# Resizing the phases and shortening the bank-by-bank tails of a streamed weight-gradient matmul, with smaller early transfers and a longer warm-up

**Chip, cores, metric.** One NeuronCore of one Trainium2 chip. The metric is the device time of one execution in microseconds (us). The "span" of a profile is the same execution seen from the core's first instruction, 1.7 to 1.8 us shorter than the device time here. All runs named below were of the fast state, with correct results.

## The reference

```python
batch, m, k, n = 16, 512, 1024, 768
input       = randn(batch, m, k)      # float32
grad_output = randn(batch, m, n)      # float32
grad_weight = einsum('bmk,bmn->kn', input, grad_output)   # float32, 1024 x 768
```

It is one matmul with a contraction over 16 x 512 = 8192 rows. Both inputs are read once, 58.7 MB of float32.

## The kernel before

The contraction is cut into 64 slices of 128 rows. A slice is x (128 x 1024) and g (128 x 768); GpSimd's DMAs cast both to bf16 on the way into SBUF (the page: 58.72 MB read from HBM, 28.97 MB moved by their queue). The output has 8 row blocks k; each is computed in a "wide" part of 512 columns, which fills one of the kernel's 8 PSUM buffers (a "bank" in the code), and a "narrow" part of 256. With 8 of them, the wide parts of all 8 blocks can stand in PSUM at once, but not the narrow ones beside them. So slices are grouped in phases: within a phase all wide matmuls come first, slice by slice as slices land ("streamed"), then the narrow ones, block by block, and each finished bank is added into an SBUF accumulator.

```python
PHASES = [4, 8, 10, 14, 18, 10]        # slices in each phase
BANKWISE = [1, 2, 4, 6, 10, 10]        # of these, the last ones done bank by bank
WARMUP = 20
# [cut: setup]
    nc.sync.dma_start(out=g0f, in_=G[0:P, 0:NA])              # slice 0 comes as float32
    nc.scalar.dma_start(out=x0f[:, 0:NA], in_=X[0:P, 0:NA])   # NA = 512
    nc.sync.dma_start(out=x0f[:, NA:K], in_=X[0:P, NA:K])
    for i in range(WARMUP):                                   # runs while slice 0 is on its way
        nc.tensor.matmul(wps[:, 0:P], warm, warm, start=(i == 0), stop=(i == WARMUP - 1))
# [cut: slice 0 is cast to bf16 by VectorE and ScalarE in blocks of 256 columns]
# [cut: slices 1 to 3: g's wide columns, x; then the narrow columns of slices 0 to 3 in one transfer]
    def load_pair(s):                                         # from slice 4 on: two slices a transfer
        gt = xg.tile([P, 2, N], bf16, name="gt")              # 20 buffers
        xt = xg.tile([P, 2, K], bf16, name="xt")
# [cut: two DMAs issued by GpSimd]
    for ph, C in enumerate(PHASES):
        load_upto(s0 + (PHASES[ph + 1] if not last else 0))
        streamed = slices[: C - BANKWISE[ph]]
        rest = slices[C - BANKWISE[ph] :]
        for i, s in enumerate(streamed):                      # wide, slice by slice
            for k in range(KS):
                nc.tensor.matmul(banks[k], xblk[s](k), gwide[s], start=(i == 0), stop=False)
        for k in range(KS):                                   # wide, bank by bank
            for i, s in enumerate(rest):
                nc.tensor.matmul(bank, xblk[s](k), gwide[s], ...)
            evacuate(acc[:, k, 0:NA], bank, ...)              # VectorE adds the bank into acc
        for k in range(KS):                                   # narrow, bank by bank
            for i, s in enumerate(slices):
                nc.tensor.matmul(bank[:, 0:NB], xblk[s](k), gnarrow[s], ...)
            evacuate(acc[:, k, NA:N], bank[:, 0:NB], ...)
```

The bankwise tail spreads the evacuations: with R slices in it, banks finish R x 0.216 us apart. Its price is that block 0 wants all R slices at once.

## Time and profile before

Device time 184.51 us in the median of three runs (184.46 to 185.03); the profiled execution took 183.78, with a span of 182.0.

| from the profile before | |
|---|---|
| wide matmul, start to start | 0.216 us |
| narrow matmul, start to start | 0.109 us |
| all matmuls, 512 wide and 512 narrow | 166.5 us |
| a pair of slices in the DMA queue | 4.31 us |
| first matmul of slice 0 | 4.98 us |
| longest waits of TensorE for a slice | near 21, 26, 30 and 121 us |
| last matmul | 178.4 us |

How to read it: a timeline row gives start, duration, engine, source line, what it writes from what, and how many instructions are merged; in square brackets the idle time before it and what ended that. A wide matmul is shown with 379 ns, but the next one starts 216 ns after it; the distance between starts is what counts. The prediction below shows the lines.

### The profile page before, as it was taken

The page shows a single profiled execution, that of the slowest core. Times are in us where ns is not written, and L with a number is a line of the kernel's source. Part 1 is how long each engine was busy: PE and PEld are TensorE (multiplying, and loading weights), DVE is VectorE, ACT ScalarE, POOL GpSimd, SP SyncE. Part 2 cuts the span into 40 slices and gives each one's busy share as a digit, 9 for nine tenths or more (in the row PEclk, how much of TensorE's full clock was granted, in tenths as well). Part 3 has the DMA queues.
Part 4 walks back from the last instruction along what each step waited for, and adds up shares of the span by engine and source line. Part 5 has one row for each costly group of instructions (what it writes and reads, how often), then busy time and mean ns, then how long its engine had stood idle before and what let it go on. Part 6 is the DMA issues. An engine that isn't in the chain of part 4 may idle for free.

```text
span 182.0 us, 2421 instructions
## 1 busy us (share of the span) xinstructions
PE 171.2 (94%) x1032; PEld 102.2 (56%) x1044; DVE 49.1 (27%) x92; ACT 5.6 (3%) x11; POOL 36.1 (20%) x71
## 2 busy tenths in 40 slices
PE   5999878999999999999999999969999999999992
PEld 4347323684435884444488844424448886444781
DVE  0126001950038430004542200013332211333331
ACT  2116000000000000000000000000000000000000
POOL 7642222222222222222222222222000000000000
PEclk9999999999999999999999999999999999999999
DMA  5999999999999999999999999999999100333342
GB/s 175 200 210 213 213 213 211 214 213 211 215 211 213 213 213 214 212 212 212 214 213 212 211 213 214 214 212 214 212 214 210 22 4 0 115 115 115 121 142 86
DMA packets 12778, 33.05 MB, mean 182 GB/s; under 512 B 1376, under 2 KB 3296, under 8 KB 12768
## 3 DMA queue, kind: packets, MB, share of 16 engines
q0 software_dynamic: 10032, 28.97, 81.0%
q1 hardware_dynamic: 2592, 3.67, 5.7%
q10 hardware_dynamic: 144, 0.26, 0.5%
q8 instruction: 8, 0.13, 0.3%
q14 instruction: 2, 0.02, 0.0%
HBM read 58.72 MB, written 3.15 MB: 340 GB/s over the span
## 4 chain that ended last, share of the span: by engine, by line
DMA 62%; PE 31%; POOL 3%; issue 2%; DVE 0%; POOLq 0%
DMA xt<-in_input_dram 62%; PE bank L145 18%; PE bank L156 13%; POOL gw L81 1%; POOL x L82 1%; POOL gn L86 0%; POOL gt L96 0%; DVE acc L122 0%; POOLq L178 0%
## 5 line engine op out<-in xcount | busy, mean ns | idle before, releaser
L122 DVE TENSOR_TENSOR acc<-bank,acc 128x512 f32<-128x512 f32 (+1 forms) x80 | 43.8, 557 | 117.6 <-PE bank L145 84.4
L145 PE MATMUL bank<-gt,xt 128*128 128x512 bf16 x251 | 56.3, 379 | 2.7 <-DMA xt<-in_input_dram 2.3
L156 PE MATMUL bank<-gt,xt 128*128 128x256 bf16 x480 | 53.2, 273 | 0.0
L139 PE MATMUL bank<-gt,xt 128*128 128x512 bf16 x218 | 48.9, 379 | 2.0 <-DMA xt<-in_input_dram 1.7
L156 PEld LDWEIGHTS <-xt 128*128 128x128 bf16 x480 | 47.0, 98 | 6.5
L145 PEld LDWEIGHTS <-xt 128*128 128x128 bf16 x256 | 24.7, 98 | 33.4 <-DMA xt<-in_input_dram 4.4
L139 PEld LDWEIGHTS <-xt 128*128 128x128 bf16 x224 | 21.8, 98 | 27.6 <-DMA xt<-in_input_dram 2.5
L97 POOL DMA_DIRECT2D xt<-in_input_dram x30 | 15.9, 531 | 49.0 <-DMA xt<-in_input_dram 47.8
L96 POOL DMA_DIRECT2D gt<-in_grad_output_dram x30 | 15.9, 531 | 40.0 <-DMA gt<-in_grad_output_dram 35.8
L117 DVE COPY acc<-bank 128x512 f32<-128x512 f32 (+1 forms) x8 | 4.1, 553 | 8.1 <-PE bank L145 7.2
L139 PEld LDWEIGHTS <-x 128*128 128x128 bf16 x24 | 2.8, 119 | 6.0 <-issue 2.8
L139 PE MATMUL bank<-g,x 128*128 128x512 bf16 x8 | 3.6, 631 | 1.6 <-ACT x L69 1.6
L139 PE MATMUL bank<-gw,x 128*128 128x512 bf16 x16 | 4.0, 408 | 0.0
L119 ACT COPY acc<-bank 128x512 f32<-128x512 f32 (+1 forms) x8 | 3.5, 486 | 9.0 <-PE bank L145 7.4
L156 PE MATMUL bank<-gn,x 128*128 128x256 bf16 x32 | 3.7, 272 | 0.0
L156 PEld LDWEIGHTS <-x 128*128 128x128 bf16 x32 | 3.1, 98 | 0.6
L64 PE MATMUL bank<-warm 128*128 128x128 bf16 x20 | 2.3, 313 | 1.1 <-DVE warm L61 1.1
L64 PEld LDWEIGHTS <-warm 128*128 128x128 bf16 x20 | 2.0, 147 | 1.1 <-DVE warm L61 1.1
L81 POOL DMA_DIRECT2D gw<-in_grad_output_dram x3 | 1.8, 594 | 0.8 <-POOLq L178 0.8
L145 PE MATMUL bank<-gw,x 128*128 128x512 bf16 x7 | 1.8, 379 | 0.1
L82 POOL DMA_DIRECT2D x<-in_input_dram x3 | 1.7, 556 | 0.0
L68 DVE CAST g<-g0f 128x512 bf16<-128x512 f32 x1 | 0.5, 477 | 3.3 <-DMA g0f<-in_grad_output_dram 3.3
(12 smaller groups left out, 4.8 us busy)
## 6 DMA issues: line engine op xcount, KB each, us to landing
xt<-in_input_dram POOLq DMA_DIRECT2D x30, 512.0 KB, 17.0
gt<-in_grad_output_dram POOLq DMA_DIRECT2D x30, 384.0 KB, 17.0
out_dram<-acc SPq DMA_DIRECT2D x8, 256.0 KB, 2.0
out_dram<-acc SPq DMA_DIRECT2D x8, 128.0 KB, 1.7
x<-in_input_dram POOLq DMA_DIRECT2D x3, 256.0 KB, 6.5
gw<-in_grad_output_dram POOLq DMA_DIRECT2D x3, 128.0 KB, 5.8
g0f<-in_grad_output_dram SPq DMA_DIRECT2D x1, 256.0 KB, 3.6
x0f<-in_input_dram ACTq DMA_DIRECT2D x1, 256.0 KB, 3.8
```

The lines of the kernel that those rows point to most:

```text
L64: nc.tensor.matmul(wps[:, 0:P], warm, warm, start=(i == 0), stop=(i == WARMUP - 1))
L68: nc.vector.tensor_copy(out=g0, in_=g0f)
L81: nc.gpsimd.dma_start(out=gt, in_=G[s * P : (s + 1) * P, 0:NA])
L82: nc.gpsimd.dma_start(out=xt, in_=X[s * P : (s + 1) * P, :])
L96: nc.gpsimd.dma_start(out=gt, in_=G[rows, :].rearrange("(p r) n -> p r n", r=2))
L97: nc.gpsimd.dma_start(out=xt, in_=X[rows, :].rearrange("(p r) k -> p r k", r=2))
L117: nc.vector.tensor_copy(out=dst, in_=src)
L119: nc.scalar.copy(out=dst, in_=src)
L122: nc.vector.tensor_add(out=dst, in0=src, in1=dst)
L139: nc.tensor.matmul(banks[k], xblk[s](k), gwide[s], start=(i == 0), stop=False)
L145: nc.tensor.matmul(bank, xblk[s](k), gwide[s], start=(i == 0 and not streamed), stop=(i == len(rest) - 1),)
L156: nc.tensor.matmul(bank[:, 0:NB], xblk[s](k), gnarrow[s], start=(i == 0), stop=(i == C - 1),)
```

## The change

The intent: let each phase take as many slices as DMA has ready by then, want no slice early, get the first slices in small pieces and in the order of need, and have the clock up when they come.

- PHASES and BANKWISE: all phases from the third on but the last keep one slice for the bankwise pass.
- Slices 1 to 11 come without their narrow columns, which follow once for each of the first two phases; slices 12 to 21 come one by one; pairs start at 22, with 14 pair buffers instead of 20.
- Slice 0's x in pieces of 256, 256 and 512 columns; 30 warm-up matmuls instead of 20.

```diff
-PHASES = [4, 8, 10, 14, 18, 10]
-
-BANKWISE = [1, 2, 4, 6, 10, 10]
-WARMUP = 20
+PHASES = [5, 7, 10, 15, 18, 9]
+
+BANKWISE = [1, 2, 1, 1, 1, 9]
+
+SPLIT = 2
+
+PAIRED = 22
+WARMUP = 30
[cut]
+    QX = 256
     g0f = head.tile([P, NA], f32, name="g0f")
-    x0f = head.tile([P, K], f32, name="x0f")
+    x0f = [head.tile([P, w], f32, name=f"x0f{i}") for i, w in enumerate((QX, QX, NA))]
     nc.sync.dma_start(out=g0f, in_=G[0:P, 0:NA])
-    nc.scalar.dma_start(out=x0f[:, 0:NA], in_=X[0:P, 0:NA])
-    nc.sync.dma_start(out=x0f[:, NA:K], in_=X[0:P, NA:K])
+    nc.scalar.dma_start(out=x0f[0], in_=X[0:P, 0:QX])
+    nc.scalar.dma_start(out=x0f[1], in_=X[0:P, QX : 2 * QX])
+    nc.sync.dma_start(out=x0f[2], in_=X[0:P, NA:K])
[cut: the casts of slice 0 read the new pieces; ScalarE's comes first]
+    def load_split(slices):
+        n = len(slices)
+        for s in slices:
+            if s == 0:
+                continue
+            gt = early.tile([P, NA], bf16, name=f"gw{s}")
+            xt = early.tile([P, K], bf16, name=f"x{s}")
+            nc.gpsimd.dma_start(out=gt, in_=G[s * P : (s + 1) * P, 0:NA])
+            nc.gpsimd.dma_start(out=xt, in_=X[s * P : (s + 1) * P, :])
[cut]
+        gn = early.tile([P, n, NB], bf16, name=f"gn{slices[0]}")
+        rows = slice(slices[0] * P, (slices[0] + n) * P)
+        nc.gpsimd.dma_start(out=gn, in_=G[rows, NA:N].rearrange("(s p) n -> p s n", p=P))
[cut]
+    def load_rows(s, R):
+        gt = xg.tile([P, R, N], bf16, name=f"gt{R}", bufs=10 if R == 1 else 14)
+        xt = xg.tile([P, R, K], bf16, name=f"xt{R}", bufs=10 if R == 1 else 14)
[cut]
+    def load_phase(ph):
[cut]
+        if ph < SPLIT:
+            load_split(list(range(loaded, loaded + PHASES[ph])))
+            loaded += PHASES[ph]
+            return
+        upto = sum(PHASES[: ph + 1])
+        while loaded < upto:
+            R = 2 if loaded >= PAIRED else 1
+            load_rows(loaded, R)
+            loaded += R
```

More of the change, by code (lines that the diff above doesn't have):

```diff
@@ L41 @@
     head = ctx.enter_context(tc.tile_pool(name="head", bufs=1))
-    xg = ctx.enter_context(tc.tile_pool(name="xg", bufs=20))
+    early = ctx.enter_context(tc.tile_pool(name="early", bufs=1))
+    xg = ctx.enter_context(tc.tile_pool(name="xg", bufs=13))
     accp = ctx.enter_context(tc.tile_pool(name="accp", bufs=1))
@@ L66 @@
     g0 = head.tile([P, NA], bf16, name="g0")
-    x0 = [head.tile([P, 256], bf16, name=f"x0_{i}") for i in range(4)]
+    x0 = [head.tile([P, QX], bf16, name=f"x0_{i}") for i in range(4)]
+    nc.scalar.copy(out=x0[0], in_=x0f[0])
     nc.vector.tensor_copy(out=g0, in_=g0f)
-    nc.scalar.copy(out=x0[0], in_=x0f[:, 0:256])
-    nc.vector.tensor_copy(out=x0[1], in_=x0f[:, 256:512])
-    nc.vector.tensor_copy(out=x0[2], in_=x0f[:, 512:768])
-    nc.scalar.copy(out=x0[3], in_=x0f[:, 768:1024])
+    nc.vector.tensor_copy(out=x0[1], in_=x0f[1])
@@ L73 @@
+    nc.vector.tensor_copy(out=x0[2], in_=x0f[2][:, 0:QX])
+    nc.scalar.copy(out=x0[3], in_=x0f[2][:, QX : 2 * QX])
     xblk[0] = lambda k: x0[k // 2][:, (k % 2) * P : (k % 2 + 1) * P]
     gwide[0] = g0[:, :]
-    C0 = PHASES[0]
-    for s in range(1, C0):
-        gt = head.tile([P, NA], bf16, name=f"gw{s}")
-        xt = head.tile([P, K], bf16, name=f"x{s}")
-        nc.gpsimd.dma_start(out=gt, in_=G[s * P : (s + 1) * P, 0:NA])
-        nc.gpsimd.dma_start(out=xt, in_=X[s * P : (s + 1) * P, :])
-        xblk[s] = lambda k, xt=xt: xt[:, k * P : (k + 1) * P]
-        gwide[s] = gt[:, :]
@@ L85 @@
-    gn = head.tile([P, C0, NB], bf16, name="gn")
-    nc.gpsimd.dma_start(
-        out=gn, in_=G[0 : C0 * P, NA:N].rearrange("(s p) n -> p s n", p=P)
-    )
-    for s in range(C0):
-        gnarrow[s] = gn[:, s, :]
-    def load_pair(s):
-        gt = xg.tile([P, 2, N], bf16, name="gt")
-        xt = xg.tile([P, 2, K], bf16, name="xt")
-        rows = slice(s * P, (s + 2) * P)
-        nc.gpsimd.dma_start(out=gt, in_=G[rows, :].rearrange("(p r) n -> p r n", r=2))
-        nc.gpsimd.dma_start(out=xt, in_=X[rows, :].rearrange("(p r) k -> p r k", r=2))
-        for r in range(2):
+    def load_split(slices):
[7 more added lines that the diff above has]
+            nc.gpsimd.dma_start(out=xt, in_=X[s * P : (s + 1) * P, :])
+            xblk[s] = lambda k, xt=xt: xt[:, k * P : (k + 1) * P]
+            gwide[s] = gt[:, :]
+        gn = early.tile([P, n, NB], bf16, name=f"gn{slices[0]}")
+        rows = slice(slices[0] * P, (slices[0] + n) * P)
+        nc.gpsimd.dma_start(out=gn, in_=G[rows, NA:N].rearrange("(s p) n -> p s n", p=P))
+        for i, s in enumerate(slices):
+            gnarrow[s] = gn[:, i, :]
@@ L99, in load_pair @@
+    def load_rows(s, R):
+        gt = xg.tile([P, R, N], bf16, name=f"gt{R}", bufs=10 if R == 1 else 14)
+        xt = xg.tile([P, R, K], bf16, name=f"xt{R}", bufs=10 if R == 1 else 14)
+        rows = slice(s * P, (s + R) * P)
+        nc.gpsimd.dma_start(out=gt, in_=G[rows, :].rearrange("(p r) n -> p r n", r=R))
+        nc.gpsimd.dma_start(out=xt, in_=X[rows, :].rearrange("(p r) k -> p r k", r=R))
+        for r in range(R):
             xblk[s + r] = lambda k, xt=xt, r=r: xt[:, r, k * P : (k + 1) * P]
@@ L101, in load_pair @@
             gnarrow[s + r] = gt[:, r, NA:N]
-    loaded = C0
-    def load_upto(n):
+    loaded = 0
+    def load_phase(ph):
         nonlocal loaded
-        while loaded < min(n, S):
-            load_pair(loaded)
-            loaded += 2
+        if ph >= len(PHASES):
+            return
+        if ph < SPLIT:
+            load_split(list(range(loaded, loaded + PHASES[ph])))
+            loaded += PHASES[ph]
+            return
+        upto = sum(PHASES[: ph + 1])
[3 more added lines that the diff above has]
+            loaded += R
     evac_count = 0
@@ L124, in evacuate @@
             nc.sync.dma_start(out=OUT[:, k, c0:c1], in_=dst)
+    load_phase(0)
     s0 = 0
@@ L130 @@
         s0 += C
-        load_upto(s0 + (PHASES[ph + 1] if not last else 0))
+        load_phase(ph + 1)
         streamed = slices[: C - BANKWISE[ph]]
```

## The prediction

> **What bounds the kernel now.** I read the page's busy shares and chain first, then the timeline of TensorE, then the list of waits, then the issues on GpSimd. The page's shares and the chain that ended last:
>
> ```profile
> PE 171.2 (94%) x1032; PEld 102.2 (56%) x1044; DVE 49.1 (27%) x92; ACT 5.6 (3%) x11; POOL 36.1 (20%) x71
> ...
> DMA 62%; PE 31%; POOL 3%; issue 2%; DVE 0%; POOLq 0%
> ```
>
> TensorE is busy nearly throughout, yet the chain runs through the loads of `input` for 62% of the span: TensorE lives from hand to mouth on slices of 128 rows until some moment, and from there its own work sets the end. The timeline of TensorE tells when (start, duration, instructions, idle before):
>
> ```profile
> 4.98 3.60 PE L139 MATMUL bank<-g,x 128*128 128x512 bf16 x8 [1.61 <-ACT x L69]
> 8.37 4.04 PE L139 MATMUL bank<-gw,x 128*128 128x512 bf16 x16
> ...
> 13.97 3.66 PE L156 MATMUL bank<-gn,x 128*128 128x256 bf16 x32
> 17.46 3.40 PE L139 MATMUL bank<-gt,xt 128*128 128x512 bf16 x15
> 21.37 3.63 PE L139 MATMUL bank<-gt,xt 128*128 128x512 bf16 x16 [0.50 <-DMA xt<-in_input_dram]
> 26.18 3.63 PE L139 MATMUL bank<-gt,xt 128*128 128x512 bf16 x16 [1.19 <-DMA xt<-in_input_dram]
> 30.46 3.63 PE L145 MATMUL bank<-gt,xt 128*128 128x512 bf16 x16 [0.65 <-DMA xt<-in_input_dram]
> 33.92 7.15 PE L156 MATMUL bank<-gt,xt 128*128 128x256 bf16 x64
> 40.91 10.52 PE L139 MATMUL bank<-gt,xt 128*128 128x512 bf16 x47
> ...
> 103.97 13.98 PE L139 MATMUL bank<-gt,xt 128*128 128x512 bf16 x62
> 117.79 1.89 PE L145 MATMUL bank<-gt,xt 128*128 128x512 bf16 x8
> 121.14 15.71 PE L145 MATMUL bank<-gt,xt 128*128 128x512 bf16 x71 [1.46 <-DMA xt<-in_input_dram]
> 136.69 15.88 PE L156 MATMUL bank<-gt,xt 128*128 128x256 bf16 x144
> 152.41 17.43 PE L145 MATMUL bank<-gt,xt 128*128 128x512 bf16 x78
> 169.67 8.90 PE L156 MATMUL bank<-gt,xt 128*128 128x256 bf16 x80
> ```
>
> A narrow matmul takes (40.91 - 33.92) / 64 = 0.109 us, a wide one (169.67 - 152.41) / 80 = 0.216 us. The whole work is 512 of each: 110.6 + 55.9 = 166.5 us. The rest of the 182.0 us is overhead, phase by phase:
> - start, until the first matmul of slice 0: 4.98;
> - slow clock: wide matmuls of phase 0 take 13.97 - 4.98 = 8.99 for 32, against 6.91: 2.1 lost. The weight loads beside them start 0.43 us apart until 9.2 us, 0.216 after;
> - waits for slices: phase 1 needs 33.92 - 17.46 = 16.46 for 64 matmuls (13.82): 2.6. Phase 2 by the same sum loses 0.3 and phase 3 0.3. Phase 4 needs 136.69 - 103.97 = 32.72 for 144 (31.10): 1.6. Together 4.9;
> - from the last matmul (178.4) to the end: 3.5.
>
> 4.98 + 166.5 + 2.1 + 4.9 + 3.5 = 182.0. The wait at 121.14 is the one that counts: phase 4 has 18 slices with the last 10 bank by bank, so its first bank already wants slices 52 and 53 after only 8 streamed slices. Whatever was lost before it would have been lost there anyway.
>
> The feeder, by GpSimd's issues (each waits for the transfer issued eight earlier to land, so its time marks a landing):
>
> ```profile
> 7.79 0.53 POOL L96 DMA_DIRECT2D gt<-in_grad_output_dram  x1 [1.27 <-DMA x<-in_input_dram]
> ...
> 9.69 0.53 POOL L96 DMA_DIRECT2D gt<-in_grad_output_dram  x1 [0.71 <-DMA x<-in_input_dram]
> ...
> 35.03 0.53 POOL L97 DMA_DIRECT2D xt<-in_input_dram  x1 [1.95 <-DMA xt<-in_input_dram]
> ...
> 39.33 0.53 POOL L97 DMA_DIRECT2D xt<-in_input_dram  x1 [1.93 <-DMA xt<-in_input_dram]
> ```
>
> The two x slices at 7.79 and 9.69 are 1.91 us apart: that is a slice without its narrow columns. A pair of whole slices takes 4.31, so 2.16 a slice, against 8 x (0.216 + 0.109) = 2.60 us of TensorE. DMA gains 0.44 us a slice on TensorE overall, but in a phase that runs only wide columns TensorE eats 1.73 us a slice, and is faster than DMA. Phases are therefore limited by the lead that DMA has built.
>
> [...] one wide matmul shows 379 ns but they start 216 ns apart, so I count starts. [...] 0.43 and 0.216, and the switch came at 9.2 us, 4.2 us after slice 0 began[...]. [...] A pair reads 1.835 MB in 4.31 us, 426 GB/s[...]: with eight in flight, a 256 KB slice of x costs 1.25 us (landings at 8.17 and 9.41) and a 512 KB pair 2.46. [...] A streamed phase holds all eight, so its narrow groups need evacuated banks.
>
> **The change part by part.**
> (a) Slice 0 in finer pieces. x's first 256 columns arrive as their own 128 KB. ScalarE's cast began at 4.52, after a 256 KB piece. Half the bytes on that queue save some 0.3 to 0.4 us (my estimate from 768 KB in about 2.4 us of transfers), so slice 0 starts near 4.6. The cast (0.40 us) stays.
> (b) Warm-up 20 to 30: ten more at 0.107 us, so issue ends near 1.06 + 3.2 = 4.3, not 3.2. The gap before slice 0 falls from 1.6 to about 0.3 us, and the clock should rise near 5 to 8 us instead of 9.2. Up to 2 us of slow clock goes; but slice 1 lands at 7.5 as before, so most of it becomes a wait for slice 1.
> (c) Narrow columns last, single slices. Landings, starting from the measured 7.51 of slice 1, by 1.91: slices 2, 3, 4 at 9.4, 11.3, 13.2; five narrow blocks (1.35 x 5/4 = 1.7) 14.9; slices 5 to 11 by 1.91 until 28.3; seven narrow blocks (2.4) 30.7. Ten single slices at about 2.2 (the pair's half[...]): slice 21 at 52.7. Then pairs by 4.31: slice 37 at 87.2, slice 55 at 126.0, slice 63 at 143.
> (d) Phases and BANKWISE. TensorE in order, with a warm clock from slice 1 on: slice 4 starts at 13.3; phase 0 ends 13.3 + 1.7 + 40 x 0.109 = 19.4. Phase 1: five streamed slices to 28.0, a 0.3 wait for slice 11, 16 x 0.216, 56 x 0.109: 37.9. Phase 2 (10 slices, 1 bankwise) wants slice 21 at 37.9 + 9 x 1.73 = 53.5; it lands at 52.7: no wait. End 63.9. Phase 3 (15) wants slice 36 at 63.9 + 14 x 1.73 = 88.1; there at 87.2: no wait. End 102.9. Phase 4 (18) wants slice 54 at 132; there at 126. End 149.7. Phase 5 (9): 23.4, end 173.2. All waits of 1.6 to 2.6 us in the middle are gone; what is left is the start.
> (e) Evacuation. With one slice bankwise, banks finish 0.216 apart but VectorE adds one in 0.69. In phase 2 bank k is free about 0.4 + 0.72 (k + 1) after that pass began; narrow group k starts at 1.7 + 1.09 k. Bank 7: 6.2 against 9.4. No wait in the longer phases; phase 1 (7 slices, 2 bankwise) has 6.4 against 8.8.
> (f) Buffers. 14 pairs instead of 20. The pair of slices 50 and 51 waits for the first pair of phase 3, free in that phase's last narrow group, about 101.5; the queue would have liked it at 100.1, and three pairs (13 us) are then still in flight. Hidden.
>
> Sum: 173.2 + 3.5 = 176.7 of span; I add 0.3 for a clock that rises late, 177.0. That is 5.0 less than 182.0, and 184.51 - 5.0 = **179.5 us**.
>
> **The rivals.**
> 1. The clock stays slow. [...] 0 to 1.3 us come back, for phases 0 and 1 have almost no slack: 179.5 to 180.8. [...] Against: DMA waits hide lateness until about 9 us.
> 2. Single slices and small descriptors cost more than 2.2 us. Slack at slice 21 is 0.8 and at slice 36 0.9, so 10% more on ten slices (2 us) becomes a wait of about 1.2 us: 180.7. [...]
> 3. VectorE becomes the bound at phase ends, TensorE stalling on banks in five phases: 1 us each would bring 184. The sums in (e) speak against it, and VectorE is at 27%.
> 4. The wait at 121 was hidden anyway. No: after it TensorE runs without a gap to the end.
>
> **Range and chances.** The ideal sum gives 179.2; each of rivals 1 and 2 costs 1.2 to 1.3, both together 181.7. Better than 178.3 needs an earlier slice 1, which nothing gives. Range 178.2 to 181.3. Over 2% faster means under 180.8: 0.78. Within 2%: 0.21. Slower: 0.01.
>
> **What would show it.** Right: TensorE's timeline has no wait for a slice longer than 0.4 us after phase 0; slice 0 starts near 4.6; slice 4 near 13.3; phase 4's narrow groups begin near 134; the last matmul is near 173. Wrong: an idle of TensorE released by VectorE (rival 3), landings of single slices over 2.3 us apart (rival 2), weight loads still 0.43 us apart beyond 9 us (rival 1), or GpSimd waiting for TensorE long enough to empty the queue (f).

## The result and the profile after

The changed kernel takes 178.62 us in the median of four runs (178.62 to 178.90), the kernel before 184.49 in the same rounds (184.12 to 185.03). Ratios here and below are the mean time of one kernel's fast runs over the mean of the other's fast runs of the same rounds, so they are not quite the ratio of the quoted medians: 0.9684, 95% interval 0.9658 to 0.9710, so 3.2% faster. The profiled execution took 178.62 with a span of 176.9.

Busy shares and the chain that ended last, from the page after:

```profile
PE 171.3 (97%) x1054; PEld 102.8 (58%) x1054; DVE 46.3 (26%) x92; ACT 5.6 (3%) x11; POOL 46.7 (26%) x90
...
PE 82%; DMA 13%; POOL 2%; issue 1%; DVE 0%; POOLq 0%
```

TensorE's busy time has not changed (171.2 and 171.3); its work is the same but for ten more warm-up matmuls, in a shorter span. The chain has turned round: TensorE's own work is 82% of it, and DMA only 13%, where it was 62%. The timeline of TensorE in the profile after:

```profile
1.06 3.38 PE L71 MATMUL bank<-warm 128*128 128x128 bf16 x30 [1.06 <-DVE warm L68]
4.62 2.39 PE L157 MATMUL bank<-g,x 128*128 128x512 bf16 x8 [0.18 <-ACT x L75]
7.48 5.73 PE L157 MATMUL bank<-gw,x 128*128 128x512 bf16 x24 [0.47 <-DMA x<-in_input_dram]
13.20 1.90 PE L163 MATMUL bank<-gw,x 128*128 128x512 bf16 x8
...
27.94 0.38 PE L163 MATMUL bank<-gw,x 128*128 128x512 bf16 x1
28.77 3.41 PE L163 MATMUL bank<-gw,x 128*128 128x512 bf16 x15 [0.45 <-DMA x<-in_input_dram]
...
38.13 15.70 PE L157 MATMUL bank<-gt,xt 128*128 128x512 bf16 x72
53.67 1.89 PE L163 MATMUL bank<-gt,xt 128*128 128x512 bf16 x8
...
88.30 1.89 PE L163 MATMUL bank<-gt,xt 128*128 128x512 bf16 x8
...
132.48 1.89 PE L163 MATMUL bank<-gt,xt 128*128 128x512 bf16 x8
134.21 15.88 PE L174 MATMUL bank<-gt,xt 128*128 128x256 bf16 x144
```

The waits near 21, 26, 30 and 121 us are gone. One wait for a slice is left after phase 0, at 28.77 (slice 11): block 0 of slice 10 began at 27.94 and took 0.216, so 0.61 us by starts. From there TensorE runs to the last matmul without a gap worth naming: 431 wide and 472 narrow ones follow, 93.1 + 51.5 us, which from 28.77 makes 173.4; the last one is at 173.3. The last-slice rows at 53.67, 88.30 and 132.48 have no idle in brackets.

The overheads by the same sums as before:

| us | before | after |
|---|---|---|
| until the first matmul of slice 0 | 4.98 | 4.62 |
| phase 0: wide part beyond 0.216 a matmul | 2.1, slow clock | 1.7, mostly waits for slices 1 to 4 |
| waits of phase 1 | 2.6 | 0.6 |
| waits of phases 2, 3, 4 | 0.3 + 0.3 + 1.6 | under 0.1 together |
| all matmuls | 166.5 | 166.5 |
| last matmul | 178.4 | 173.3 |
| from there to the end | 3.5 | 3.5 |

The clock rose at 5.65 us after the span's start (the trace's clock record), against 9.20 before.

### The profile page after: what moved, and what is told of

Same layout as the page of the kernel before. It is cut to its first block, busy times and chain, and to the rows that moved or that the text cites. A ratio compares the mean times of both kernels' runs of the same rounds, so it can differ in the third digit from the quotient of the medians.

```text
span 176.9 us, 2469 instructions
## 1 busy us (share of the span) xinstructions
PE 171.3 (97%) x1054; PEld 102.8 (58%) x1054; DVE 46.3 (26%) x92; ACT 5.6 (3%) x11; POOL 46.7 (26%) x90
## 4 chain that ended last, share of the span: by engine, by line
PE 82%; DMA 13%; POOL 2%; issue 1%; DVE 0%; POOLq 0%
PE bank L157 39%; PE bank L174 29%; PE bank L163 14%; DMA x<-in_input_dram 13%; POOL gw L91 1%; POOL x L92 1%; DVE acc L139 0%; POOLq L196 0%
## 5 line engine op out<-in xcount | busy, mean ns | idle before, releaser
L139 DVE TENSOR_TENSOR acc<-bank,acc 128x512 f32<-128x512 f32 (+1 forms) x80 | 41.1, 552 | 113.4 <-PE bank L163 88.5
L157 PE MATMUL bank<-gt,xt 128*128 128x512 bf16 x320 | 69.6, 379 | 0.0
L157 PEld LDWEIGHTS <-xt 128*128 128x128 bf16 x320 | 31.3, 98 | 37.1
L174 PE MATMUL bank<-gt,xt 128*128 128x256 bf16 x416 | 46.1, 273 | 0.0
L174 PEld LDWEIGHTS <-xt 128*128 128x128 bf16 x416 | 40.7, 98 | 5.6
L163 PE MATMUL bank<-gt,xt 128*128 128x512 bf16 x96 | 21.4, 379 | 0.0
L163 PEld LDWEIGHTS <-xt 128*128 128x128 bf16 x96 | 9.4, 98 | 11.1 <-DMA xt<-in_input_dram 0.2
L157 PE MATMUL bank<-gw,x 128*128 128x512 bf16 x64 | 14.5, 380 | 0.5 <-DMA x<-in_input_dram 0.5
L157 PEld LDWEIGHTS <-x 128*128 128x128 bf16 x72 | 6.7, 99 | 10.2 <-DMA x<-in_input_dram 2.0
L174 PE MATMUL bank<-gn,x 128*128 128x256 bf16 x96 | 10.8, 273 | 0.0
L174 PEld LDWEIGHTS <-x 128*128 128x128 bf16 x96 | 9.4, 98 | 1.5 <-DMA gn<-in_grad_output_dram 0.3
L91 POOL DMA_DIRECT2D gw<-in_grad_output_dram x11 | 6.1, 551 | 4.3 <-DMA x<-in_input_dram 3.1
L92 POOL DMA_DIRECT2D x<-in_input_dram x11 | 6.0, 547 | 4.2 <-DMA x<-in_input_dram 2.7
L163 PE MATMUL bank<-gw,x 128*128 128x512 bf16 x24 | 5.7, 380 | 0.5 <-DMA x<-in_input_dram 0.5
L163 PEld LDWEIGHTS <-x 128*128 128x128 bf16 x24 | 2.2, 98 | 3.8 <-DMA x<-in_input_dram 1.4
L157 PE MATMUL bank<-g,x 128*128 128x512 bf16 x8 | 2.4, 452 | 0.2 <-ACT x L75 0.2
```

The source lines that it names most:

```text
L91: nc.gpsimd.dma_start(out=gt, in_=G[s * P : (s + 1) * P, 0:NA])
L92: nc.gpsimd.dma_start(out=xt, in_=X[s * P : (s + 1) * P, :])
L139: nc.vector.tensor_add(out=dst, in0=src, in1=dst)
L163: nc.tensor.matmul(bank, xblk[s](k), gwide[s], start=(i == 0 and not streamed), stop=(i == len(rest) - 1),)
L174: nc.tensor.matmul(bank[:, 0:NB], xblk[s](k), gnarrow[s], start=(i == 0), stop=(i == C - 1),)
```

## The experiments

**The theory** is the reckoning of the prediction: slices land at times that DMA sets; the end is the last moment at which TensorE had to wait, plus all the work left then. An edit earlier than that moment is worth nothing; an edit that moves the moment is worth what the next binding landing allows. **The rivals**: the head (clock and slice 0) carries the gain; or the sizes of the transfers do; or the phase sizes do, with BANKWISE a mere companion. Twelve kernels were run, in three groups of four, each group on one chip beside the kernel before (medians 184.03, 184.06 and 184.06). In the one-part runs, "the kernel before" and "the changed kernel" say from which side the edit was made.

### BANKWISE alone, on the kernel before

```diff
-BANKWISE = [1, 2, 4, 6, 10, 10]
+BANKWISE = [1, 2, 1, 1, 1, 10]
```

> The kernel before with one change: BANKWISE [1, 2, 1, 1, 1, 10]. Reckoning theory: the waits of phases 2 to 4 (0.3 + 0.3 + 1.6 us before) go, because the last slices are wanted later; phase 1's 2.6 us and the slow clock's 2.1 us stay, as they are now not hidden behind a later wait. Last matmul near 176.2 instead of 178.4, span near 179.8, time near 182.3 (1.2% faster than before). Rival, that the single-slice transfers and the phase sizes carry the gain and BANKWISE is only their companion: no change, 184.5.

Measured: 181.56 (181.53 to 181.89), ratio 0.9869 (0.9849 to 0.9888). Its timeline of TensorE:

```profile
30.54 3.63 PE L145 MATMUL bank<-gt,xt 128*128 128x512 bf16 x16 [0.66 <-DMA xt<-in_input_dram]
...
132.74 1.89 PE L145 MATMUL bank<-gt,xt 128*128 128x512 bf16 x8
```

The wait for slices 10 and 11 at 30.54 stands where it stood; the last slice of phase 4 is done at 132.74 without a wait. 2.4 us came from one line, against 2.2 reckoned. The rival that BANKWISE is a companion is out. In this profile the clock rose only at 10.9 us and phase 0 ended late, yet the wait at 30.54 was still the one that bound.

### The head alone, on the kernel before

The edit is the head of the change (pieces of slice 0, 30 warm-up matmuls) and nothing else.

> The kernel before with the head alone: slice 0 in finer pieces and 30 warm-up matmuls. Reckoning theory: slice 0 starts near 4.6 instead of 5.0 and the clock rises near 5.7 instead of 9.2, phase 0 ends about 0.9 us earlier, but the wait for slice 52 at 121.1 swallows all of it: within 0.3 us of before, 184.5. Rival, that the head carries the gain (clock 2.1 + start 0.4): 182.0.

Measured: 183.99 against 184.03, ratio 1.0001 (0.9988 to 1.0014; 14 and 19 runs). The timeline:

```profile
7.39 3.81 PE L141 MATMUL bank<-gw,x 128*128 128x512 bf16 x15
...
22.14 3.63 PE L141 MATMUL bank<-gt,xt 128*128 128x512 bf16 x16 [1.63 <-DMA xt<-in_input_dram]
...
121.34 15.71 PE L147 MATMUL bank<-gt,xt 128*128 128x512 bf16 x71 [1.38 <-DMA xt<-in_input_dram]
```

Slice 1 starts at 7.39 instead of 8.37, and slice 6 waits 1.63 us instead of 0.50. The wait at 121 is where it was. About 1 us won in phase 0 became 1 us of waiting in phase 1. The rival that the head carries the gain is out, for this kernel.

### The changed kernel without its head

Both parts of the head back to the old ones in the changed kernel.

> The changed kernel with the old head (x of slice 0 in two pieces of 512 columns, 20 warm-up matmuls). Reckoning theory: slice 0 starts near 5.0 with a slow clock to about 9.2; slices 1 to 4 then run without waits, and phase 0 ends 0.8 us later, but the wait for slice 11 (0.6 to 0.8 us in the changed kernel) takes most of it back: 0.2 to 0.5 us over the changed kernel, 178.9 to 179.1; if the clock rises later than 9.2, up to 1.5 more. Rival, that the head is worth its full 2.5 us: 181.1.

Measured: 179.40 (178.83 to 179.66), ratio to before 0.9741 (0.9721 to 0.9761), on another chip than the first run of the changed kernel (0.9684) and its repeat below (0.9697). So here the same edit is worth about 0.45 to 0.6%, 0.8 to 1.0 us; the intervals of this run and of the first run do not meet, those of this run and the repeat just do. That is more than the 0.2 to 0.5 expected and inside the "later clock" clause. The profiled execution was the fastest of the four (178.83), with the clock rising at 7.67; that the other three had a later clock is one possible cause, and late landings as in the next run are another; neither is shown, since only the profiled one has a trace.

### The changed kernel again, and each part of the head by itself

The next three runs and the last one of the study shared a chip.

> The changed kernel itself, beside the next three on one chip. Every theory: 178.3 to 178.9, ratio to before 0.968 to 0.971. Its profile shows when the clock rises: between 4.3 and 6.8 us, as in five of six profiles with 30 warm-up matmuls.

Measured: 178.57 in the median, five runs of 178.44 to 178.67 and one, the profiled, of 179.39; ratio 0.9697 (0.9671 to 0.9723). The clock rose at 5.57, as expected. The profile is that of the long execution:

```profile
8.17 5.72 PE L157 MATMUL bank<-gw,x 128*128 128x512 bf16 x23 [1.23 <-DMA x<-in_input_dram]
...
38.38 15.70 PE L157 MATMUL bank<-gt,xt 128*128 128x512 bf16 x70
54.42 1.90 PE L163 MATMUL bank<-gt,xt 128*128 128x512 bf16 x8 [0.34 <-DMA xt<-in_input_dram]
```

Slice 1 was ready at 8.17 instead of 7.48, but that isn't what made it long: at 38.38 TensorE was only 0.25 us behind the first profile. Slice 21 set the end. It came at 54.4, where in the first profile it was there before it was wanted at 53.7, and from there all is 0.75 later. The landings had fallen 1.0 us further behind at one point: at 42.27 the last of a transfer's 16 semaphore increments in the trace (the last one completes its landing) came 1.21 us after the one before it, right behind a 16 KB transfer of the instruction queue at 40.16; (c) below returns to these. The same kernel's profiles thus differ by as much as some edits here are worth.

```diff
-WARMUP = 30
+WARMUP = 20
```

> The changed kernel with 20 warm-up matmuls, the fine pieces kept. Theory of the late clock: the profiles with 20 had it rise at 7.7, 9.2 and 10.9 us. Up to 9.2 costs nothing to 0.1 us, since TensorE only loses its waits for slices 1 to 4 and 11; at 11 us it costs 1. So 0.2 to 0.8 us over the changed kernel in the median, 178.8 to 179.4, with more spread between runs than the changed kernel. Rival, that the pieces of slice 0 made what the old head cost: no difference.

Measured: 178.78 (178.52 to 179.04), ratio 0.9703 (0.9677 to 0.9729): 0.2 us over the repeat in the median, within the intervals. The clock rose at 7.44 in its profile. Not told apart from nothing.

The second part, pieces of 512 columns with 30 warm-up matmuls (the diff of the head's DMAs and casts, reversed):

> The changed kernel with x of slice 0 in two pieces of 512 columns, 30 warm-up matmuls kept. Reckoning theory: slice 0 starts 0.3 to 0.4 us later, all of it taken from the wait for slice 1: within 0.2 us of the changed kernel. If the longer gap behind the warm-up matmuls delays the clock to 9 us in some runs, those are up to 0.5 us longer. Rival, that the pieces are worth their 0.4 us: 179.0.

Measured: 179.06 (178.67 to 179.45), ratio 0.9713 (0.9687 to 0.9739): 0.5 over the repeat in the median, again within the intervals. The profiled execution had the late clock of the second clause. Its weight loads, which here start with the matmuls they serve (the first of both at 5.22):

```profile
5.22 0.13 PEld L155 LDWEIGHTS <-x 128*128 128x128 bf16 x2 [1.05 <-ACT x L74]
...
9.47 0.15 PEld L155 LDWEIGHTS <-x 128*128 128x128 bf16 x1 [0.28 <-issue]
9.89 0.15 PEld L155 LDWEIGHTS <-x 128*128 128x128 bf16 x1 [0.28 <-issue]
10.29 1.61 PEld L155 LDWEIGHTS <-x 128*128 128x128 bf16 x8 [0.25 <-issue]
```

They come one by one, 0.42 us apart, until 10.29, although 30 warm-up matmuls ran; slice 0 came 1.05 us after the last warm-up load, against 0.44 in the first profile of the changed kernel, where the clock rose at 5.65. The fine pieces and the longer warm-up can be read as two ways of keeping that gap short; no run shows that they need each other.

What decides when the clock rises is not shown; the gap alone does not. With 30 warm-up matmuls, TensorE's timeline has it idle before slice 0 for 0.72, 0.76 and 0.78 us in the three profiles with a late clock (the last run of the study, the old tails below, this run), where slice 0's eight matmuls then took 3.6 us. It has 0.73 in the head alone and 0.99 with pairs from slice 12 on (below), where slice 0's last six took 1.47, so 0.22 apart. No run sets the gap.

### Pairs from slice 12 on

```diff
-PAIRED = 22
+PAIRED = 12
```

(with 19 pair buffers in place of 10 single and 14 pair ones)

> The changed kernel with pair transfers from slice 12 on (19 pair buffers, the same memory). Reckoning theory: pairs move slightly faster, but slice 20 then lands with slice 21, about 0.8 us after TensorE wants it: a wait of 0.8 us in phase 2, no wait at slice 36: 0.6 to 0.8 us over the changed kernel, 179.3. Rival, that transfer size costs per byte and single slices lose (2.2 against 2.16 us a slice): 0.4 us under the changed kernel.

Measured: 179.41 (179.33 to 179.94), ratio 0.9752 (0.9734 to 0.9770), 1.0 to 1.2 us over the changed kernel by the ratios. The timeline shows the wait that was expected, at slice 20:

```profile
52.78 1.90 PE L157 MATMUL bank<-gt,xt 128*128 128x512 bf16 x8 [0.56 <-DMA xt<-in_input_dram]
```

By starts it is 52.78 - 38.25 - 64 x 0.216 = 0.7 us, and the profiled span is 0.8 us longer than the changed kernel's. Single slices here are not about bandwidth (they cost 2.20 us a slice, a pair 4.31, so 0.05 a slice more): they let the first of two slices be used when it lands. The rest of the measured difference, 0.2 to 0.4, is not explained; in this profile slice 0 started at 5.43 and slice 11 was there 0.1 later too.

### Narrow columns last in phase 0 only

```diff
-SPLIT = 2
+SPLIT = 1
```

(with 17 single buffers)

> The changed kernel with narrow columns last in phase 0 only (SPLIT = 1; slices 5 to 11 come as whole single slices). Reckoning theory: a slice of phase 1 then costs 2.2 us of DMA instead of 1.91, slice 11 lands near 30.8 instead of 28.7, and TensorE waits about 2.7 us in phase 1 instead of 0.8: about 2.0 us over the changed kernel, 180.6. Rival, that the order of columns within a phase doesn't matter since the bytes are the same: 178.6.

Measured: 180.79 (180.64 to 180.89), ratio 0.9821 (0.9806 to 0.9835), 2.2 to 2.5 us over the changed kernel (by the medians or the ratios).

```profile
31.02 3.41 PE L163 MATMUL bank<-gt,xt 128*128 128x512 bf16 x15 [1.81 <-DMA xt<-in_input_dram]
```

Slice 11 is used at 31.02 instead of 28.77, 2.25 us later, and the whole rest with it. The bytes are the same; their order is worth 2.2 us.

### The old tails in the new phases

```diff
-BANKWISE = [1, 2, 1, 1, 1, 9]
+BANKWISE = [1, 2, 4, 6, 10, 9]
```

> The changed kernel with the old tails, BANKWISE [1, 2, 4, 6, 10, 9]. Reckoning theory: phase 2 wants slice 21 after six streamed slices and waits about 4 us for slices 20 and 21, phase 3 waits about 3.4 us for slice 36, phase 4 about 0.6 us for slice 54: last matmul near 181.4 instead of 173.2, time near 186.7, slower than before. Rival, that the phase sizes carry the gain by themselves: under 180.

Measured: 186.55 (186.40 to 186.95), ratio 1.0140 (1.0120 to 1.0159): slower than before, as expected. The phases of the change are sized so that the last slice of each lands just before TensorE wants it last; wanted earlier, it isn't there. The timeline has the waits, and one thing that was not expected:

```profile
51.09 0.39 PE L163 MATMUL bank<-gt,xt 128*128 128x512 bf16 x1 [1.80 <-DMA xt<-in_input_dram]
53.31 3.46 PE L163 MATMUL bank<-gt,xt 128*128 128x512 bf16 x8 [1.84 <-DMA xt<-in_input_dram]
...
87.97 9.45 PE L163 MATMUL bank<-gt,xt 128*128 128x512 bf16 x42 [1.19 <-DMA xt<-in_input_dram]
```

Eight wide matmuls took 3.46 us from 53.31, where eight took 1.89 in the changed kernel (at 53.67): about half speed. The stretches of the same profile (time, TensorE busy, granted clock, DMA share, GB/s) agree:

```profile
48.50:53.40 4.90, 1.26 (x6) 1.00 1.13 212
53.40:56.90 3.50, 3.38 (x8) 0.51 1.06 212
```

After two waits, of 1.80 and 1.84 us with one matmul between them, the granted clock was 0.51 for 3.5 us. The lateness was then paid back at slice 36, which was waited for 1.2 us instead of the 3.4 expected, so the sum still came out: the last matmul at about 181.2 against 181.4 reckoned.

### One bankwise slice in phase 1, and a further step

```diff
-BANKWISE = [1, 2, 1, 1, 1, 9]
+BANKWISE = [1, 1, 1, 1, 1, 9]
```

> The changed kernel with one bankwise slice in phase 1 too (BANKWISE[1] = 1). Reckoning theory: the wait for slice 11 (0.6 to 0.8 us) goes, since TensorE works on slice 10 meanwhile, but slices 21 and 36 land when they did and are now waited for (0.1 + 0.4 us), and VectorE's adds may hold the last banks of phase 1 by up to 0.4 us: within 0.2 us of the changed kernel, 178.5. Rival, that the wait for slice 11 is the only one that binds: 177.9.

Measured: 178.26 (177.97 to 178.59), ratio 0.9685 (0.9666 to 0.9704). The wait for slice 11 went, and no wait of TensorE for VectorE came. In the profiled execution slice 1 was ready only at 8.05, so TensorE reached slices 21 and 36 after they had landed and the give-back wasn't seen. Not told apart from the changed kernel.

```diff
-PHASES = [5, 7, 10, 15, 18, 9]
-BANKWISE = [1, 2, 1, 1, 1, 9]
+PHASES = [5, 8, 9, 14, 18, 10]
+BANKWISE = [1, 1, 1, 1, 1, 10]
```

(with 9 single buffers in place of 10)

> A further step: PHASES [5, 8, 9, 14, 18, 10], BANKWISE [1, 1, 1, 1, 1, 10], the rest as in the changed kernel. Reckoning theory: TensorE works on slice 10 while slice 11 comes, and slices 21 and 35 land 1 us before they are wanted, so the waits after phase 0 go but for 0.2 us for the narrow columns of phase 1: last matmul near 172.9 instead of 173.2 to 173.4, 0.3 to 0.5 us under the changed kernel, 178.2. If VectorE's adds hold banks at the end of phase 1: 178.6.

Measured: 178.53 (178.05 to 179.08), ratio 0.9700 (0.9676 to 0.9724). Its profile has no wait for data after slice 1, of 1.15 us, and phase 0's small ones; the waits in the middle are all gone. The kernel is no faster all the same. The profile puts it down to slice 1, which came at 8.05, 0.57 later than in the changed kernel's profile, so that what is left hangs on the first transfers; the other three executions have no trace.

The last run goes on from it: the x of slices 1 to 4 in two transfers each, and the narrow columns of the first two phases in two.

```diff
+            parts = 2 if slices[0] == 0 else 1
+            w = K // parts
+            xs = [early.tile([P, w], bf16, name=f"x{s}_{i}") for i in range(parts)]
+            for i, xt in enumerate(xs):
+                nc.gpsimd.dma_start(out=xt, in_=X[rows, i * w : (i + 1) * w])
[cut]
+        for part in (slices[:-2], slices[-2:]):
```

> The further step (PHASES [5, 8, 9, 14, 18, 10], one bankwise slice in each phase) with the x of slices 1 to 4 in two transfers of 512 columns, and the narrow columns of each of the first two phases in two transfers, the last two slices apart. Reckoning theory: in the further step only slices 1 to 4 were waited for, each whole; with halves TensorE works on the first half while the second lands, 0.6 us earlier[...]: 0.4 to 0.5 us under the further step and 0.4 to 0.8 under the changed kernel on the same chip, near 178.0. If slice 12 or the narrow columns then bind: 0.2 less gain.

Measured: 178.25 in the median, four runs of 177.90 to 178.32 and two of 179.4; ratio 0.9688 (0.9654 to 0.9723), against 0.9697 for the changed kernel on the same chip. Four runs are where the theory put them, but the two long ones widen the interval over both, so a gain is not shown. That 0.4 to 0.5 of the halves' 0.6 us would be left was the author's estimate. The profiled execution is one of the long ones: slice 0 at 5.16, the clock at 10.4, and no wait for any of slices 1 to 4, which halves can't help then.

## Why the prediction was right

The forecast was 179.5 with 178.2 to 181.3; measured 178.62, faster, with the span at 176.9 against 177.0 forecast. That the span fits to 0.1 is in part luck: the sum had 176.7 plus 0.3 for a clock that rises late; the clock did not rise late in this profile, and the wait for slice 11 took 0.3 more than reckoned. Of the signs named, one failed narrowly: no wait for a slice after phase 0 was to be longer than 0.4, and that for slice 11 shows 0.45 (0.6 by starts). The others held: phase 4's narrow matmuls began at 134.21, the last matmul was at 173.3.

- *Which wait counts.* Confirmed from both sides: taking that wait away by one line gave 2.4 us, and improving what lies before it (the head alone) gave 0.0.
- *(a), slice 0.* It started at 4.62, forecast 4.6. In other profiles with the same pieces it started between 4.55 and 5.43, so the step's size is not settled. Its worth by itself was not resolved.
- *(b), the clock.* It rose at 5.65, forecast 5 to 8; that a shorter gap brings it up earlier was the author's estimate. That slice 1 would limit what this is worth held: it was ready at 7.48, forecast 7.5.
- *(c), landings.* Slices 2 to 4 as forecast; slice 4 began at 13.20 (13.3). Slice 11 came at 28.7, forecast 28.3, and slice 36 at 88.1, forecast 87.2; the slack of 0.9 at slice 36 was 0.2. The term that was mis-sized is the landing of slice 7. GpSimd's issues of x in the profile after, each marking a landing:

```profile
17.01 0.53 POOL L92 DMA_DIRECT2D x<-in_input_dram  x1 [0.71 <-DMA x<-in_input_dram]
...
18.92 0.53 POOL L92 DMA_DIRECT2D x<-in_input_dram  x1 [0.73 <-DMA x<-in_input_dram]
...
21.39 0.53 POOL L92 DMA_DIRECT2D x<-in_input_dram  x1 [1.26 <-DMA x<-in_input_dram]
```

  The first two are 1.91 apart, the next 2.47. In the trace, the landing behind the last one has 15 of its 16 increments by 20.54 and the last at 21.11, and a 16 KB transfer of the instruction queue ran from 18.61 for 0.94 us. The trace has eight such transfers (queue q8 of the page, 0.13 MB); beside this one 0.5 us of a full queue was lost, and the lag stayed in all later landings. A second one at 82.8 stands before the late slice 36, with another 0.5. Not each such transfer costs as much: those at 39.8 and 61.5 left no lag, while in the changed kernel's second profile the first four cost 0.2, 1.0, 0 and 0. The increments suggest why. Before the one at 39.8 a single increment of the 16 was 0.58 late, after it (at 42.08) two were, 0.03 apart. GpSimd's next issue follows the last increment (21.11, then 21.39), so a delay to another of the 16 would add nothing. No run varied this; it is argued from the times.
- *(d), phases.* Phase ends at 19.3, 38.1, 64.1, 103.1 and 149.9, forecast 19.4, 37.9, 63.9, 102.9 and 149.7. The difference from phase 1 on is the wait for slice 11, 0.6 instead of 0.3.
- *(e), VectorE.* No wait of TensorE for a bank, with the evacuations in tails of one slice; also not with one in phase 1. Rival 3 is out.
- *(f), buffers.* GpSimd did wait for TensorE, and longer than reckoned. From the issues after:

```profile
97.04 0.53 POOL L106 DMA_DIRECT2D xt<-in_input_dram  x1 [1.98 <-DMA xt<-in_input_dram]
102.17 0.53 POOL L105 DMA_DIRECT2D gt<-in_grad_output_dram  x1 [4.59 <-PE bank L174]
```

  The transfer eight earlier had landed at 98.6, so it cost 3.3 us, not 1.4. Landings went on 4.3 us apart all the same: hidden, as forecast.
- *Rivals 1 and 2.* Single slices came 2.20 us apart (slices 12 to 21 from 33.3 to 53.1), as forecast. A pair of slices reads 426 GB/s of float32 (1.835 MB in 4.31 us); written as bf16 it is half of that, and the page shows 213 GB/s. With eight transfers in flight, 256 KB of x (as written in bf16) took 1.25 us and 512 KB 2.46 in the profile before, so the smaller size cost under 2%. What sets the rate is not shown by any run. The late clock didn't happen in this profile; with 30 warm-up matmuls it did in three others, at 9.1, 10.2 and 10.4. The last two are executions of 179.45 and 179.41, 0.8 to 0.9 over the changed kernel's median on that chip and inside the 0 to 1.3 of rival 1, but slice 0 was late in them as well (5.22 and 5.16).
- *From span to time.* This step made most of the 0.9 us by which the forecast was too high. I subtracted the saved span from the median of 184.51, but the span belonged to an execution of 183.78, and profiled pairs lie 1.7 to 1.8 apart (183.78 and 182.0; 178.62 and 176.9). 177.0 + 1.75 would have given 178.8.

What stays open: what the new phase sizes are worth by themselves, since no run put the old PHASES beside the new tails and transfers (that they don't carry the gain alone, the run with the old tails shows); how the 0.8 to 1.0 us of the head in the changed kernel divide between warm-up and pieces, and what makes the first transfers of an execution 0.6 us early or late.

## What to carry to other kernels

Find the last moment at which the busiest engine waits for data, and value every edit by whether it moves that moment: the same head was worth nothing in one kernel and 0.8 to 1.0 us, measured across chips, in the other. Where compute is faster than the loads in one part of a phase and slower in the other, size the phase by landing times and ask for the last slice last; order and granularity of the same bytes were worth 2.2 and 0.7 us here. Reckon in starts and landings taken from the trace, and add the distance between span and time of the same execution.
